# Three results of layer 0's small projections take their buffers from the mixer's rings instead of the ring of raw weights

## The chip, the cores and the metric

The kernel runs on one core of one Trainium2 chip. The metric is the time of one execution in microseconds (us); each kernel's figure is a median of several runs. Before the change it is 3133.64 us (three runs, 3126.05 to 3135.7).

## The reference

A two-layer encoder trunk over 1024 time steps and 1024 channels, all in float32. Layer 0 mixes with two recurrent head groups, layer 1 with banded attention; after each comes an MLP and a gated embedding. The change lies in layer 0's mixer. This is what matters of it:

```python
h = rmsnorm(x, norm_mix_g[i]); proj = h @ even_w_in[e]; dh = token_shift(h) - h
xw, xa, xg = [h + dh * mu_lora[j] for j in range(3)]
w_log = -softplus(-(w0 + tanh(xw @ w1) @ w2)) - 0.5          # rwkv decay
a = sigmoid(a0 + (xa @ a1) @ a2);  g = sigmoid(xg @ g1) @ g2
beta = sigmoid(beta_logit)                                    # columns of proj, 4 heads
gd = -exp(a_log) * softplus(alpha_logit + dt_bias)            # columns of proj, 4 heads
```

The products `xw @ w1`, `xa @ a1` and `xg @ g1` are the low-rank ("lora") products. Since `dh` is a shifted `h` minus `h`, each is computed as `h @ ((1 - mu) * w)` plus the shifted result of `h @ (mu * w)`. The second of these is the "second low-rank product".

## The kernel before, in words

**Tiling.** Channels lie on the 128 partitions, time on the free axis, and layer 0 takes time in two halves of 512 steps. A dense product is 8 blocks of 128 input channels; each block is three TensorE matmuls of 128x512 (high weights by high and low activations, then low weights by high activations), so a product is 24 matmuls into one PSUM bank (`dps`; `dense_part`, L324). Its evacuation multiplies by the row scale on VectorE.

**Weights.** A raw weight tile is 128x1024 and comes by a DMA on SP's queue (L297). `split_w` (L300) turns it into a high part on ScalarE (`whi`, L303) and a low part on VectorE (`wlo`, L304). Raw tiles have the tag `wraw` in the pool `wp`, a ring of **two** slots. A new tile takes the older slot, and what writes it waits until the last reader of the tile there is done.

**Units.** `l0_in` (L567 on) runs 16 units u: four rwkv and four delta-net ("gdn") units in turn for each half. A unit has three or four dense products for its projections, whose results go to the ring `raw` (six slots). In the first unit of each half (u = 0 and u = 8) come in addition, in this order of code: the low-rank pair `la` (decay and a), after the projections `gdn_scalars` (the eight beta and decay logits) and the low-rank pair `lg` (gate). `lora` (L684) loads `lraw`, multiplies it on GpSimd by `1 - mu` and by `mu` (L697, two `wraw` tiles), splits both, and runs two dense products. The second goes through `project` (L670) into `sb`; GpSimd adds it to the first (L706). `gdn_scalars` (L709) clears a `wraw` tile on GpSimd (L712), loads the eight columns, splits, runs a product of which 8 rows count (`ba`, L715), transposes `ba` on TensorE (L192), and computes beta and the decay `gs_g` on VectorE in about thirty small steps (L722 to L749). The cumulative sums (`gdn_cum`, L759) need `gs_g`.

**The chain of a unit.** `rwkv_front` (L799): mixes of raw with its shifted self (`mix`, L807 on ScalarE and L808 on VectorE), two small matmuls from `lao` (`tp`), tanh (L826 and L828), scan (L833), exponentials, `AR` (L864), `Bt` (L865), then score matmuls, then their scaling into `N` on ScalarE (L883), and `inverse_start`, whose substitution runs on GpSimd after two trips through DRAM (L396 to L418). `rwkv_front` takes its temporaries from the ring `f` (11 slots).

**What sets the order.** A planner (`run`, with the table `LAT`) interleaves the generators and so sets the order of emission; its inputs do not change here. Then the framework's scheduler, which simulates the program, fixes the order on each engine. Each engine runs its instructions in that order, and an instruction that waits holds all that stand behind it on its engine. A ring's slots decide what an instruction may wait for, so moving a tile from one ring to another changes waits and, by the scheduler, the order.

Of the kernel before, what the change touches and what calls it, by code (L numbers as in the profile page):

```python
# [8 lines left out]
F32 = mybir.dt.float32  # L9
# [8 lines left out]
P = 128  # L18
# [91 lines left out]
class Trunk:  # L110
# [573 lines left out]
    def lora(self, i, mus, key):  # L684

        nc, a = self.nc, self.a
        om, _ = _VOFF["mulora"]
        raw = self.wp.tile([P, 1024], F32, tag="wraw", name="lraw")
        nc.sync.dma_start(out=raw, in_=a["lora1"][i])

        ws = []
        for src in (self.dv["omul"], self.vecs[:, om:om + 24]):
            w = self.wp.tile([P, 1024], F32, tag="wraw", name="wraw")
            wv = w.rearrange("p (k c) -> p k c", k=NK)
            rv = raw.rearrange("p (k c) -> p k c", k=NK)
            for (c0, c1, j) in mus:
                nc.gpsimd.tensor_tensor(wv[:, :, c0:c1], rv[:, :, c0:c1],  # L697
                                        src[:, 8 * j:8 * j + 8].rearrange("p (k o) -> p k o", o=1)
                                        .broadcast_to((P, NK, c1 - c0)), op=ALU.mult)
            ws.append(w)  # L700
        out = (self.l0 if key == "lg" else self.fr).tile([P, HB], F32, tag=key + "o", name=key + "o", bufs=2 if key == "lg" else 1)
        wa, wb = [self.split_w(w) for w in ws]
        yield from self.dense_half(wa, lambda ps: nc.vector.tensor_tensor(out, ps, self.rs, op=ALU.mult))
        sb = self.wp.tile([P, 1024], F32, tag="wraw", name="sb")
        yield from self.project(wb, key, 1, raw=sb)
        nc.gpsimd.tensor_tensor(out, out, sb[:, 0:HB], op=ALU.add)  # L706
        return out

    def gdn_scalars(self, hf, sc):  # L709
        nc, a, l0 = self.nc, self.a, self.l0  # L710
        raw = self.wp.tile([P, 1024], F32, tag="wraw", name="wraw")
        nc.gpsimd.memset(raw, 0.0)  # L712
        nc.sync.dma_start(out=raw.rearrange("p (k c) -> p k c", k=NK)[:, :, 0:8], in_=a["wba"])
        ba = self.wp.tile([P, 1024], F32, tag="wraw", name="ba")
        yield from self.dense_half(self.split_w(raw), lambda ps: nc.vector.tensor_tensor(ba[0:8, 0:HB], ps[0:8], self.rs[0:8],  # L715
                                                                                         op=ALU.mult))
        yield "gdn_scalars0"
        pt = self.bank()
        for i in range(4):
            self.tr(pt[:, 8 * i:8 * i + 8], ba[0:8, i * P:(i + 1) * P], self.ident[0:8, 0:8])  # L720
        bat = self.sm.tile([P, 4, 8], F32, tag="bat", name="bat")
        nc.vector.tensor_copy(bat.rearrange("p i c -> p (i c)"), pt[:, 0:32])  # L722
        sh = [P, 4, 4]

        def new(nm):
            return self.sm.tile(sh, F32, tag="gs_" + nm, name="gs_" + nm)
        sc["beta"] = new("beta")
        nc.scalar.activation(sc["beta"], bat[:, :, 0:4], AF.Tanh, scale=0.5)
        V = nc.vector
        V.tensor_scalar(sc["beta"], sc["beta"], 0.5, 0.5, op0=ALU.mult, op1=ALU.add)  # L730
        y, ab, u = new("y"), new("ab"), new("u")
        V.tensor_tensor(y, bat[:, :, 4:8], self.hv[:, 1:2, :].broadcast_to(sh), op=ALU.add)

        V.tensor_scalar(ab, y, -1.0, None, op0=ALU.mult)
        V.tensor_tensor(ab, y, ab, op=ALU.max)
        nc.scalar.activation(u, ab, AF.Exp, scale=-1.0)
        V.tensor_scalar(ab, u, 2.0, None, op0=ALU.add)
        V.reciprocal(ab, ab)
        s, s2, poly = new("s"), new("s2"), new("poly")
        V.tensor_tensor(s, u, ab, op=ALU.mult)  # L740
        V.tensor_tensor(s2, s, s, op=ALU.mult)
        V.tensor_scalar(poly, s2, 2.0 / 17, 2.0 / 15, op0=ALU.mult, op1=ALU.add)
        for n in (13, 11, 9, 7, 5, 3, 1):
            V.tensor_tensor(poly, poly, s2, op=ALU.mult)
            V.tensor_scalar(poly, poly, 2.0 / n, None, op0=ALU.add)
        V.tensor_tensor(poly, poly, s, op=ALU.mult)
        V.scalar_tensor_tensor(poly, y, 0.0, poly, op0=ALU.max, op1=ALU.add)
        sc["g"] = new("g")
        V.scalar_tensor_tensor(sc["g"], poly, -1.0, self.ea.broadcast_to(sh), op0=ALU.mult, op1=ALU.mult)  # L749
        self.mark(("g", hf), self.lat["gdn_scalars1"])  # L750
# [1351 lines left out]
```

## Time and profile before

| | before |
|---|---|
| median of the runs | 3133.64 us |
| the profiled execution | 3130.04 us, of which the span is 3128.3 us |
| TensorE busy, clock granted | 3000.5 us (96%), 0.968 |
| VectorE, ScalarE, GpSimd busy | 2234.1 us, 1510.6 us, 532.5 us |
| layer 0's mixer | about 0 to 880 us of the span |
| its tail with the MLP | about 880 to 1700 us |
| attention | about 1700 to 2300 us |
| second tail | about 2300 to 3128 us |

Rows of a timeline give start, length, engine, line, operation, output and inputs, shape, count, and in brackets the idle time just before and what ended it. A "PEld" is a weight load, which overlaps matmuls. Line numbers are those of the kernel before; after L704 the changed kernel's are one lower.

### The profile page before, as it was taken

The numbers are of one execution on the slowest core, as the hardware profiler recorded it, in microseconds if no ns is written. First come the engines' busy times: TensorE is split into PE (matmuls) and PEld (weight loads), VectorE is DVE, ScalarE is ACT, GpSimd is POOL, SyncE is SP. The second block draws the span as 40 slices with busy tenths as digits, with TensorE's granted clock in tenths as the row PEclk, the third lists the DMA queues.
The fourth block names the chain that finished last, engine by engine and source line by source line (L and its number), as shares of the span: only waits on it lengthen the run. The fifth ranks groups of instructions, "written<-read, shape, count | busy, mean of one in ns | idle before, by whom it ended". The sixth has DMA issues, their size and how long they took to land.

```text
span 3128.3 us, 47113 instructions
## 1 busy us (share of the span) xinstructions
PE 3000.5 (96%) x17288; PEld 2476.6 (79%) x17288; DVE 2234.1 (71%) x4518; ACT 1510.6 (48%) x2922; POOL 532.5 (17%) x978
## 2 busy tenths in 40 slices
PE   7999999999999999999999898999899999999999
PEld 5777777777777788888888888988888788888887
DVE  6646675667758688888866576777768788888862
ACT  4323442434426544444433577777766544444431
POOL 6524443434510000000005210111110000000002
PEclk8989999999999999999999999999999999999999
DMA  3212112212346444754433211110156444654433
GB/s 130 77 43 69 47 44 79 63 56 64 105 159 205 151 152 148 247 177 151 130 108 118 68 36 33 46 35 19 67 181 205 152 155 148 239 182 149 135 107 103
DMA packets 187639, 358.45 MB, mean 115 GB/s; under 512 B 45712, under 2 KB 47888, under 8 KB 187408
## 3 DMA queue, kind: packets, MB, share of 16 engines
q1 hardware_dynamic: 158608, 303.00, 29.9%
q10 hardware_dynamic: 28800, 52.44, 4.4%
q8 instruction: 136, 2.23, 0.3%
q14 instruction: 95, 0.78, 0.1%
HBM read 262.04 MB, written 93.32 MB: 114 GB/s over the span
## 4 chain that ended last, share of the span: by engine, by line
PE 79%; DVE 10%; ACT 4%; DMA 3%; issue 2%; POOL 1%; SPq 0%; DVEq 0%; ACTq 0%; POOLq 0%
PE dps L177 67%; PE ch L177 2%; PE pm L177 1%; PE po L177 1%; PE tp L177 1%; PE iz L177 1%; DVE ptile L350 1%; PE pt L192 1%; DVE f L1058 1%; PE sn L177 1%; PE py L177 1%; DVE pb L1942 1%; ACT pb L1955 1%; DVE wlo L304 1%; POOL subt L415 1%
## 5 line engine op out<-in xcount | busy, mean ns | idle before, releaser
L177 PE MATMUL dps<-r,act 128*128 128x512 f32 x3528 | 831.5, 393 | 0.0
L177 PEld LDWEIGHTS dps<-r,act 128*128 128x128 f32 x3528 | 665.0, 189 | 146.7
L177 PE MATMUL dps<-xg,whi 128*128 128x512 f32 x1280 | 439.1, 424 | 16.6 <-ACT xg L352 7.4
L1599 POOL TENSOR_TENSOR pn<-pn,prs 128x512 f32<-128x512 f32 x32 | 45.5, 1424 | 1578.2 <-ACT prs L386 1481.8
L177 PE MATMUL dps<-wq,act 128*128 128x384 f32 x1536 | 306.3, 345 | 7.7 <-DVE vs L1851 3.7
L177 PEld LDWEIGHTS dps<-xg,whi 128*128 128x128 f32 x1280 | 238.1, 198 | 67.8 <-ACT xg L352 7.4
L177 PEld LDWEIGHTS dps<-wq,act 128*128 128x128 f32 x1536 | 267.2, 192 | 12.1 <-DVE vs L1851 6.1
L177 PE MATMUL dps<-xg,wlo 128*128 128x512 f32 x640 | 261.5, 410 | 1.9 <-DVE wlo L304 1.9
L177 PE MATMUL dps<-late,act 128*128 128x512 f32 x960 | 229.3, 392 | 0.0
L177 PEld LDWEIGHTS dps<-late,act 128*128 128x128 f32 x960 | 180.3, 188 | 39.7
L1272 ACT CAST act<-act 128x512 fp32r<-128x512 f32 (+1 forms) x223 | 137.7, 648 | 129.5 <-PE dps L177 67.4
L1375 DVE TENSOR_TENSOR late<-late,dps 128x512 f32<-128x512 f32 x224 | 152.3, 684 | 62.1 <-PE dps L177 53.7
L1272 ACT CAST act<-late 128x512 fp32r<-128x512 f32 x210 | 124.3, 618 | 136.2 <-PE dps L177 89.3
L177 PE MATMUL dps<-act 128*128 128x512 f32 x672 | 165.2, 392 | 0.0
L1273 DVE TENSOR_TENSOR act<-act 128x512 fp32r<-128x512 f32 (+1 forms) x223 | 155.0, 722 | 5.9 <-ACT act L1272 5.7
L303 ACT CAST whi<-wraw 128x1024 fp32r<-128x1024 f32 x78 | 81.6, 1047 | 154.1 <-PE dps L177 90.3
L177 PEld LDWEIGHTS dps<-xg,wlo 128*128 128x128 f32 x640 | 125.9, 197 | 33.2 <-DVE wlo L304 4.1
L1273 DVE TENSOR_TENSOR act<-late,act 128x512 fp32r<-128x512 f32 x210 | 141.3, 687 | 11.2 <-ACT act L1272 9.3
L177 PEld LDWEIGHTS dps<-act 128*128 128x128 f32 x672 | 126.2, 188 | 28.7
L1507 DVE TENSOR_TENSOR xw<-xw,dps 128x512 f32<-128x512 f32 x174 | 118.0, 683 | 32.4 <-PE dps L177 32.2
L177 PE MATMUL dps<-xw,act 128*128 128x512 f32 x576 | 138.5, 391 | 0.0
L1380 ACT ACTIVATE late<-late 128x512 f32<-128x512 f32 x128 | 80.2, 629 | 118.4 <-DVE late L1375 112.0
(484 smaller groups left out, 5656.2 us busy)
## 6 DMA issues: line engine op xcount, KB each, us to landing
hb<-late ACTq DMA_DIRECT2D x168, 256.0 KB
act<-hb SPq DMA_DIRECT2D x138, 256.0 KB
late<-in_w SPq DMA_DIRECT2D x60, 512.0 KB
wraw<-in_w_in SPq DMA_DIRECT2D x56, 512.0 KB
act<-in_w SPq DMA_DIRECT2D x96, 256.0 KB
braw<-hb SPq DMA_DIRECT2D x72, 256.0 KB
wraw<-in_w_out SPq DMA_DIRECT2D x21, 512.0 KB
wraw<-in_w_qkv SPq DMA_DIRECT2D x21, 512.0 KB
```

What stands on the lines that cost most here:

```text
L177: return self.begin(self.nc.tensor.matmul(out, lhsT, rhs, start=start, stop=stop, skip_group_check=again))
L192: return self.begin(self.nc.tensor.transpose(out, in_, ident))
L303: nc.scalar.copy(hi, raw)
L304: nc.vector.tensor_tensor(lo, raw, hi.bitcast(F32), op=ALU.subtract)
L350: nc.vector.tensor_tensor(dst[:, 1, sl], src, dst[:, 0, sl].bitcast(F32), op=ALU.subtract)
L415: E.tensor_tensor(o, X[:, 0:i, i:i + 1].broadcast_to((NP, i, n)), Bq[:, i:i + 1, i + 1:16].broadcast_to((NP, i, n)), op=ALU.mult)
L1272: A.copy(hi, s)
L1273: V.tensor_tensor(lo, s, hi.bitcast(F32), op=ALU.subtract)
L1375: V.tensor_tensor(r, t, u, op=ALU.add)
L1380: A.activation(t, t, AF.Relu)
L1507: V.tensor_tensor(x[n][:, hs[hf]], x[n][:, hs[hf]], ps, op=ALU.add)
L1599: G.tensor_tensor(pn, pn, prs[:, sl], op=ALU.mult)
```

## The change

```diff
@@ lora
         wa, wb = [self.split_w(w) for w in ws]
         yield from self.dense_half(wa, lambda ps: nc.vector.tensor_tensor(out, ps, self.rs, op=ALU.mult))
-        sb = self.wp.tile([P, 1024], F32, tag="wraw", name="sb")
-        yield from self.project(wb, key, 1, raw=sb)
+        sb = yield from self.project(wb, key, 1)
         nc.gpsimd.tensor_tensor(out, out, sb[:, 0:HB], op=ALU.add)
@@ gdn_scalars
-        ba = self.wp.tile([P, 1024], F32, tag="wraw", name="ba")
+        ba = self.t2()
```

`sb` becomes a tile of the ring `raw` (513 columns, six slots), `ba` one of the ring `f` (11 slots). In each half the ring `wraw` so has three tiles fewer (`sb` of `la`, `ba`, `sb` of `lg`), the ring `raw` two more, the ring `f` one more. No instruction is added or removed.

The scheduler then orders the program anew. From the first instruction to the product of the logits TensorE's order is the same. Behind it, still in unit 0, stand these rows. On **TensorE** (`tp<-lao` the matmuls from the first low-rank pair, `ba` and later `f` the logits, `hsel` a column sum for unit 0), before:

```order
L177 MATMUL tp<-lao,wa_292 128x512 x2
L192 MATMUL dps<-ident,ba 128x8 x4
L177 MATMUL tp<-hsel,f 128x2 x4
L177 MATMUL dps<-xg,whi 128x512 x2
L177 MATMUL dps<-xg,wlo 128x512
```

and now:

```order
L177 MATMUL tp<-lao,wa_292 128x512 x2
L177 MATMUL tp<-hsel,f 128x2 x4
L192 MATMUL dps<-ident,f 128x8 x4
L177 MATMUL dps<-xg,whi 128x512 x2
L177 MATMUL dps<-xg,wlo 128x512
```

The transposes of the logits still stand ahead of the first product of `lg` (`dps<-xg`), behind `hsel` now. On **VectorE** at the same place (evacuation of the logits L715, now L714; the rest but `gs_` is unit 0's chain), before:

```order
L808 TENSOR_SCALAR f<-raw,vecs,f 128x512
L678 TENSOR_TENSOR sb<-dps,rsbc 128x512
L715 TENSOR_TENSOR ba<-dps,rsbc 8x512
L722 COPY bat<-dps 128x32
L732 TENSOR_TENSOR gs_y<-bat,hv 128x16
L734 TENSOR_SCALAR gs_ab<-gs_y 128x16
L829 TENSOR_SCALAR f<-f 128x512
```

and now, from the splits of both `lg` weights on:

```order
L304 TENSOR_TENSOR wlo<-wraw,whi 128x1024 x2
L853 TENSOR_SCALAR cc<-tp 128x8
L828 TENSOR_SCALAR f<-f 128x512
L854 RECIPROCAL cc<-cc 128x8
L832 TENSOR_SCALAR L<-ones,f 128x128 x4
L835 TENSOR_SCALAR m<-L 128x4
L843 TENSOR_TENSOR L<-L,m 128x516
...
L863 TENSOR_SCALAR AR<-f,E 128x4x128
L714 TENSOR_TENSOR f<-dps,rsbc 8x512
L807 TENSOR_SCALAR f<-raw,vecs,f 128x512
L721 COPY bat<-dps 128x32
```

The evacuation of the logits has moved behind unit 0's chain up to `AR`, and all `gs_` steps behind that. On **ScalarE**, where unit 0's scores are scaled into `N`, before:

```order
L894 COPY bh<-f 128x512
L303 COPY whi<-wraw 128x1024
L883 ACTIVATE N<-tp,cc 128x128 x8
L774 ACTIVATE gs_egc<-gs_gc 128x16
L776 ACTIVATE gs_ekd<-gs_gl 128x16
```

and now:

```order
L893 COPY bh<-f 128x512
L735 ACTIVATE gs_u<-gs_ab 128x16
L882 ACTIVATE N<-tp,cc 128x128 x8
L303 COPY whi<-wraw 128x1024
L906 COPY b<-tp 128x512
```

The split of unit 1's first weight (`whi`) stood ahead of `N` and stands behind it now. The splits of the `lg` weights moved up as well: one stands ahead of `tanh` of `lao`, the other between the two tanh of unit 0 (L825 and L827). On SP's queue the load of `lg`'s `lraw` stood behind three loads of `x` and stands ahead of them now, and unit 1's first weight follows those three. On GpSimd the two multiplications for `lg` moved up among the sums of squares (L665), ahead of unit 0's `k2` (now L858); and the copy that starts unit 1's third `raw` tile (L676), which needs the slot of unit 0's second, also stands ahead of `k2`, with two L665 between.

Outside unit 0 the order changes throughout the rest of layer 0's mixer and, in the same kind of small swaps, in the attention, none of whose code is touched; TensorE's order in the first tail is the same.

## The prediction

> **What bounds the kernel now.** I read the page first, then the stages, then the start of layer 0, where the edited tiles live.
>
> ```profile
> span 3128.3 us, 47113 instructions
> PE 3000.5 (96%) x17288; PEld 2476.6 (79%) x17288; DVE 2234.1 (71%) x4518; ACT 1510.6 (48%) x2922; POOL 532.5 (17%) x978
> PE 79%; DVE 10%; ACT 4%; DMA 3%; issue 2%; POOL 1%; SPq 0%; DVEq 0%; ACTq 0%; POOLq 0%
> ```
>
> TensorE (PE) bounds the kernel: 96% busy, 79% of the chain that ended last. So an edit pays only where it shortens PE's idle time or raises its clock. By stretch (PE first, clock after the engines):
>
> ```profile
> 0.00:85.00 85.00, 63.66 (x262) 48.94 (x263) 50.47 (x95) 35.33 (x63) 48.57 (x111) 0.86 0.36 120
> 85.00:880.00 795.00, 765.20 (x6413) 590.21 (x6412) 518.88 (x1172) 304.02 (x637) 333.14 (x734) 0.93 0.22 68
> 395.00:531.00 136.00, 130.37 (x1094) 100.03 (x1093) 89.47 (x220) 48.18 (x101) 55.97 (x116) 0.93 0.20 58
> 1700.00:2300.00 600.00, 545.79 (x3350) 507.95 (x3349) 418.54 (x1308) 417.09 (x972) 92.12 (x90) 0.97 0.16 53
> ```
>
> The first 85 us leave PE idle for 21.3 us; the second half's place of the same code (395 to 531) for 5.6 of 136; attention for 54.2. Two gaps of the start touch the ring of raw weights:
>
> ```profile
> 48.47 1.05 PE L177 MATMUL tp<-hsel,f 128*128 128x2 f32 x8 [0.43 <-ACT f L826]
> 55.42 1.22 PE L177 MATMUL dps<-xg,whi 128*128 128x512 f32 x2 [5.90 <-ACT whi L303]
> 57.26 0.80 PE L177 MATMUL dps<-xg,wlo 128*128 128x512 f32 x1 [0.62 <-DVE wlo L304]
> 67.08 0.49 PE L177 MATMUL py<-AR,Sh 128*128 128x128 f32 x2
> 72.48 1.22 PE L177 MATMUL tp<-bh,blkr 128*128 128x512 f32 x2 [4.91 <-ACT N L883]
> 76.08 1.20 PE L177 MATMUL dps<-xg,whi 128*128 128x512 f32 x2
> ```
>
> Gap one (5.9 us) waits for the first `lg` weight. Gap two (4.9 us) waits for `N`. What stood before them on the other queues:
>
> ```profile
> 47.13 0.42 SPq L689 DMA_DIRECT2D lraw<-in_lora  x1
> 52.38 1.92 POOL L697 TENSOR_TENSOR wraw<-lraw,d_omul 128x1024 f32<-128x1024 f32 x1 [3.05 <-DVE L L844]
> 54.33 1.04 ACT L303 CAST whi<-wraw 128x1024 fp32r<-128x1024 f32 x1 [2.47 <-POOL wraw L697]
> 66.74 6.28 SPq L297 DMA_DIRECT2D wraw<-in_w_in  x2
> 70.34 1.04 ACT L303 CAST whi<-wraw 128x1024 fp32r<-128x1024 f32 x1 [6.18 <-DMA wraw<-in_w_in]
> 71.30 2.17 ACT L883 ACTIVATE N<-tp,cc 128x128 f32<-128x128 f32 x8
> ```
>
> Gap one is `lraw` (issued at 47.13), multiplied at 52.38, split at 54.33. Gap two is ScalarE standing 6.2 us on a weight that SP could only ask for at 66.74, when the second `lg` weight had left its slot, with `N` queued behind. Each gap also costs clock afterwards:
>
> ```profile
> 50.00:52.00 2.00, 0.00 (x0) 0.00 (x0) 2.00 (x11) 0.42 (x2) 0.00 (x0) 0.50 1.00 387
> 62.00:64.00 2.00, 2.00 (x7) 1.52 (x7) 2.00 (x3) 0.46 (x1) 1.59 (x3) 0.65 0.00 0
> 64.00:66.00 2.00, 2.00 (x18) 1.49 (x18) 2.00 (x6) 0.16 (x1) 0.67 (x1) 1.00 0.00 0
> 78.00:80.00 2.00, 2.00 (x6) 1.59 (x5) 0.00 (x0) 0.00 (x0) 0.00 (x0) 0.50 0.11 11
> 80.00:82.00 2.00, 2.00 (x13) 1.75 (x12) 0.00 (x0) 0.19 (x1) 0.00 (x0) 0.88 0.23 22
> ```
>
> The granted clock is 0.50 soon after PE stops and full again only between 62 and 64, and between 80 and 82: about 6 us after dense work came back at 57.26, about 5 after 76.08.
>
> **The change, part by part.** Nothing is added or removed, so the sum is made of waits and order.
>
> *Gap one.* Three tiles leave the two-slot ring. The second `lraw` no longer waits behind `ba`'s predecessors, and on SP it now precedes three loads of `x`; both its products and splits then lie before 50 us. But the transposes of the logits stand ahead of the product that wants these weights, and their evacuation now stands on VectorE behind unit 0's chain up to `AR`. So the wait changes its name. How long it lasts comes from these rows:
>
> ```profile
> 46.67 0.68 DVE L715 TENSOR_TENSOR ba<-dps,rsbc 8x512 f32<-8x512 f32 x1 [4.75 <-PE dps L177]
> 47.73 0.69 ACT L826 ACTIVATE f<-tp,d_ha 128x512 f32<-128x512 f32 x1 [1.68 <-PE tp L177]
> 48.31 0.68 ACT L828 ACTIVATE f<-tp,d_hw 128x512 f32<-128x512 f32 x1
> 50.05 1.36 DVE L833 TENSOR_TENSOR_SCAN L<-ones,f 128x128 f32<-128x128 f32 x4
> 51.75 0.63 DVE L844 TENSOR_TENSOR L<-L,m 128x516 f32<-128x516 f32 x1
> 52.51 2.06 DVE L857 TENSOR_SCALAR f<-f,d_hka,d_omka 128x512 f32<-128x512 f32 x1
> 54.65 1.42 DVE L954 SCALAR_TENSOR_TENSOR Sh<-Sr,ee,blk 128x128 f32<-128x128 f32 x1
> 56.00 1.21 DVE L304 TENSOR_TENSOR wlo<-wraw,whi 128x1024 fp32r<-128x1024 f32 x1
> 57.13 0.41 DVE L860 TENSOR_SCALAR f<-f 128x512 f32<-128x512 f32 x1
> 59.25 0.68 DVE L864 SCALAR_TENSOR_TENSOR AR<-f,E 128x512 f32<-128x512 f32 x1
> ```
>
> ScalarE's first tanh starts at 47.73 as now; a split of 1.04 follows it, so the split of VectorE (1.21) ends at about 50.6. Behind it stand a few column steps (about 0.5 together), a 0.41 (the first `f`), the scan 1.36, `m` about 0.2, 0.63, three copies of about 0.15, L857, L954, a 0.41 and `AR` 0.68. L857 is the same kind of instruction as L860 (0.41) and took 2.06 beside GpSimd's multiplication; L954 is a quarter of `AR`'s size and took 1.42. With 0.41 and 0.35 for these two `AR` ends near 55.6, with the rows as they are near 58.3. The evacuation adds 0.68 and the transposes about 0.4: PE's dense work returns between 56.7 and 59.4, against 57.26 now, with 1.2 us of it done ahead of that. GpSimd stands at that time at the copy for unit 1's third `raw` tile, which waits for the mix behind the evacuation, so little runs beside VectorE. I take 57, a **loss of 1 us** (bounds: 0.6 to 3.4).
>
> The rows also show the pair directly:
>
> ```profile
> 38.26 1.29 POOL L665 TENSOR_TENSOR acc<-acc,xr 128x512 f32<-128x512 f32 x1
> 38.29 2.35 DVE L304 TENSOR_TENSOR wlo<-wraw,whi 128x1024 fp32r<-128x1024 f32 x1 [1.01 <-ACT whi L303]
> ```
>
> A split that began with a GpSimd addition took 2.35 instead of 1.21. The Trainium skill, "SBUF — State Buffer", section "Who interferes with whom", says that a VectorE instruction with two SBUF inputs and a GpSimd one that reads SBUF exclude each other for a whole instruction. By that rule, with GpSimd standing at its copy, the lower bound holds; by the rows alone either could. The trace agrees with the rule.
>
> *The copy that holds GpSimd.* Its queue holds two additions (1.29 each) and `k2`, so `k2` comes about 57.5 + 0.2 + 2.6 + 1.3 = 61.6, and `Bt`, which follows on VectorE, near 63. PE needs it for the scores only after 22 matmuls of `lg`: at the half clock about 9 us, with recovery as now near 63 about 8 us, so near 65. The copy is hidden by the dense work; without that cover it would cost some 4 us.
>
> *Gap two.* PE's scores come about 1 us later than now, so `py` ends near 68.6. `N` no longer stands behind the weight's split: it starts with the scores, at about 67, lasts 2.17 and frees the bank near 69.2. The 4.9 us become about 0.6. What is late next is `gs_g`: PE needs it ahead of the second `lg` product, and its chain of small steps now stands behind everything of unit 0.
>
> ```profile
> 73.12 0.17 DVE L749 SCALAR_TENSOR_TENSOR gs_g<-gs_poly,ea 128x16 f32<-128x16 f32 x1
> ```
>
> Some 25 steps of about 0.17 to 0.2 us one after the other are 5 us; from about 66.5 they end near 72, just when PE has finished the matmuls between (`tp<-bh` 1.2, the two `pm` and `cent` about 2). Bounds: ready at 71 to 74. The second `lg` product then starts near 73 instead of 76.08: a **gain of 3 us** (0.5 to 4.5, the loss at gap one being in it).
>
> *Clock.* Now the product from 76.08 runs its first 4 us at 0.50, which loses 2 us. With a gap below 1 us, or two of about 1 us among small matmuls, between nothing and all of this goes: I take **1 us** (0 to 2). The Trainium skill, "TensorE: Matmul & The Clock Gate", section "The HAM clock gate", has the clock fall after about 3.4 us without work and return after about 3.4 us of it. By that rule all 2 us would be gained and the total would be 1 us lower; the trace's recovery was slower, 5 to 6 us, so I go by the rows.
>
> *Unit 1 on.* Its first weights are loaded and split well before 73, so the dense stream goes on; unit 0's substitution starts from an `N` that is 4 us earlier. The lead of 4 us is kept.
>
> *Second half.* The same three tiles leave the ring at u = 8, where PE idles only 5.6 us in 136: **1 us** of gain (-2 to 3).
>
> *The rest of the order.* In layer 0 after 85 us PE idles 29.8 us, in attention 54.2. The swaps there have no direction that I can read off: **0**, with bounds of a fifth of these 84 us either way, that is 17.
>
> Sum against the profiled execution's 3130.04: -3 - 1 - 1 = -5, so 3125. The median shown, 3133.64, lies 3.6 above that execution; against it the forecast is **3128.6**.
>
> **The rivals.** (1) *The lead grows*: no clock loss after either gap, `AR` without any neighbour, and the second half gives its 3: 4.5 + 2 + 3, and some 4 us from the swaps, is 13.5, so 3120. For it: both gaps do start at this ring. Against: gap one stays. (2) *The swaps in attention cost more than the start gains.* PE waits there for the probabilities:
>
> ```profile
> PE po L177 <- ACT ptile L349: 7.8, 10, 1.8
> PE pt L192 <- DVE ptile L350: 5.2, 12, 1.0
> ```
>
> In the new order pairs of transposes stand in places directly behind the scores, with fewer dense matmuls between. If PE's 54.2 us of idle time there rise by two fifths (22 us), the total is +17, so 3150. It decides from 14.4 us on (5 given back and 9.4 more). For it: each such wait is about 0.5 to 0.8 us, and thirty more would do. Against: matmuls were moved both ways. (3) *The change does nothing for PE*: gap one takes its upper bound, `gs_g` comes at 74, and the second half gives nothing: -0.5, so 3133.
>
> **How the numbers follow.** A measurement of this kernel can tell about 0.3% (9.4 us) from no change. Chances: forecast 0.40, (1) 0.22, (2) 0.30, (3) 0.08. So faster 0.22, same 0.48, slower 0.30. The predicted time is 3128.6; its own case spans 3124 to 3138. The range takes in most of (1) and (2): 3112 to 3154.
>
> **What would show it.** Right: `lraw` of `lg` issued before 40; PE's wait at gap one put down to the logits' evacuation or its transposes, with dense work back near 57; no wait for `N` above 1.5 us; the second `lg` product at 72 to 74; `gs_g` near 72. Wrong: dense work back after 60, a wait for `gs_g` above 2 us, or the clock at 0.50 between 74 and 80. If the total differs by more than 9 us with a start as forecast, the stretch 1700 to 2300 or 85 to 880 holds the difference as idle time or clock of PE.

## The result, and the profile after

The changed kernel takes **3119.79 us** (median of five runs, 3115.08 to 3121.0); five runs of the kernel before beside it have a median of 3133.64 (3126.05 to 3136.78). The ratio is 0.9963 with a 95% interval of 0.9949 to 0.9977: **faster by 0.37%**, some 12 to 14 us. A second comparison with the same code (`again`, below) gave 0.9951 (0.9933 to 0.9970). The forecast was 3128.6, the size is that of rival (1).

From the page of the changed kernel, whose profiled execution took 3119.22 us:

```profile
span 3117.5 us, 47104 instructions
PE 2998.6 (96%) x17288; PEld 2477.6 (79%) x17288; DVE 2222.7 (71%) x4518; ACT 1512.2 (49%) x2922; POOL 534.0 (17%) x978
PE 81%; DVE 9%; ACT 4%; DMA 3%; issue 1%; POOL 1%; SPq 0%; DVEq 0%; POOLq 0%; ACTq 0%
```

TensorE's busy time is the same within 2 us, and the span is 10.8 us shorter. By stretch, as before:

```profile
0.00:85.00 85.00, 66.51 (x284) 51.50 (x285) 49.37 (x97) 37.03 (x64) 56.39 (x118) 0.90 0.41 132
85.00:880.00 795.00, 765.05 (x6435) 591.08 (x6433) 512.01 (x1171) 305.38 (x637) 326.13 (x728) 0.93 0.22 68
395.00:531.00 136.00, 130.46 (x1138) 102.94 (x1138) 86.62 (x217) 49.13 (x101) 51.84 (x108) 0.93 0.19 56
1700.00:2300.00 600.00, 549.41 (x3369) 511.64 (x3369) 419.81 (x1321) 420.88 (x980) 88.75 (x87) 0.96 0.17 56
```

In the first 85 us TensorE is idle 18.5 us where it was 21.3, and its clock is 0.90 instead of 0.86. Attention has 50.6 us of idle time where it had 54.2.

**Gap one** first. On TensorE:

```profile
50.13 1.05 PE L177 MATMUL tp<-hsel,f 128*128 128x2 f32 x8
59.92 0.59 PE L192 MATMUL dps<-ident,f 8*128 8x8 f32 x4 [8.74 <-DVE f L714]
60.44 1.22 PE L177 MATMUL dps<-xg,whi 128*128 128x512 f32 x2
```

The wait is now put down to the logits' evacuation (L714), as forecast, but it lasts 8.7 us where it was 5.9. On the other queues, in order of the cause:

```profile
33.54 0.35 SPq L689 DMA_DIRECT2D lraw<-in_lora  x1
49.35 1.89 POOL L697 TENSOR_TENSOR wraw<-lraw,vecs 128x1024 f32<-128x1024 f32 x1
51.28 1.05 ACT L303 CAST whi<-wraw 128x1024 fp32r<-128x1024 f32 x1 [1.21 <-POOL wraw L697]
52.36 1.32 DVE L304 TENSOR_TENSOR wlo<-wraw,whi 128x1024 fp32r<-128x1024 f32 x1 [5.47 <-ACT whi L303]
53.68 1.40 DVE L828 TENSOR_SCALAR f<-f 128x512 f32<-128x512 f32 x1
57.48 0.54 DVE L856 TENSOR_SCALAR f<-f,d_hka,d_omka 128x512 f32<-128x512 f32 x1
58.00 0.34 DVE L953 SCALAR_TENSOR_TENSOR Sh<-Sr,ee,blk 128x128 f32<-128x128 f32 x1
58.60 0.69 DVE L863 SCALAR_TENSOR_TENSOR AR<-f,E 128x512 f32<-128x512 f32 x1
59.20 0.67 DVE L714 TENSOR_TENSOR f<-dps,rsbc 8x512 f32<-8x512 f32 x1
```

`lraw` is asked for at 33.5 instead of 47.1. But GpSimd multiplies it for the second weight only at 49.35, behind sums of squares and the low-rank addition, and VectorE stands 5.47 us at the split of that weight with unit 0's chain and the evacuation queued behind. From the split's end (53.68) to that of `AR` (59.29) it takes 5.6 us where my lower end had 5.0: L857 (now L856) takes 0.54 and L954 (now L953) 0.34, as that end had it, but L828 takes 1.40 instead of 0.41.

**Gap two** is gone:

```profile
69.69 2.18 ACT L882 ACTIVATE N<-tp,cc 128x128 f32<-128x128 f32 x8 [2.89 <-PE tp L177]
71.35 0.71 PE L177 MATMUL tp<-bh,blkr 128*128 128x512 f32 x2
72.70 0.17 DVE L748 SCALAR_TENSOR_TENSOR gs_g<-gs_poly,ea 128x16 f32<-128x16 f32 x1
74.25 0.71 PE L177 MATMUL dps<-xg,whi 128*128 128x512 f32 x2
```

and the clock there, by slices as before:

```profile
74.00:76.00 2.00, 2.00 (x13) 1.69 (x12) 1.12 (x4) 1.09 (x4) 0.00 (x0) 1.00 0.21 31
```

TensorE waits no more for `N` (no bracket at 71.35), `gs_g` is there 1.0 us before its matmuls (73.89), and the second `lg` product runs at the full clock from 74.25, where it ran at half from 76.08. That full clock belongs to this profile: in two other profiles of the changed kernel (`again` and `after_d`, below) the product begins earlier, at 72.84 and 73.18, and the clock from 74 to 76 us is 0.55 and 0.61.

### The profile page after: what moved, and what is told of

Read it like the earlier page. It is cut to its first block, busy times and chain, and to the rows that moved or that the text cites. A ratio compares the mean times of both kernels' runs of the same rounds, so it can differ in the third digit from the quotient of the medians.

```text
span 3117.5 us, 47104 instructions
## 1 busy us (share of the span) xinstructions
PE 2998.6 (96%) x17288; PEld 2477.6 (79%) x17288; DVE 2222.7 (71%) x4518; ACT 1512.2 (49%) x2922; POOL 534.0 (17%) x978
## 4 chain that ended last, share of the span: by engine, by line
PE 81%; DVE 9%; ACT 4%; DMA 3%; issue 1%; POOL 1%; SPq 0%; DVEq 0%; POOLq 0%; ACTq 0%
PE dps L177 68%; PE ch L177 2%; PE po L177 2%; PE iz L177 1%; PE pm L177 1%; PE tp L177 1%; PE pt L192 1%; DVE ptile L350 1%; PE py L177 1%; PE sn L177 1%; DVE pb L1941 1%; ACT pb L1954 1%; PE pp L177 1%; DMA wraw<-in_w_out 1%; PE st L177 1%
## 5 line engine op out<-in xcount | busy, mean ns | idle before, releaser
L1374 DVE TENSOR_TENSOR late<-late,dps 128x512 f32<-128x512 f32 x224 | 152.3, 684 | 62.5 <-PE dps L177 54.2
```

Of the source, the lines that this page charges most:

```text
L1374: V.tensor_tensor(r, t, u, op=ALU.add)
```

## How the lead is followed through the program

A time at the end doesn't say where it was won. The evacuations of layer 0's dense products come in a fixed order, so the start of the same evacuation in two traces gives the lead (how much earlier it comes) at that point. One reading is good to a few us only, since the work around an evacuation is ordered anew: the changed kernel's first profile reads 4.2 at 102.6 us, -1.2 at 109.0 and 2.6 at 128.4. This table is worked out from VectorE's rows, in us against the first profile of the kernel before, at the times given there. The later columns are experiments, told below. The last two rows are span, and time at the half clock from the trace's clock records (about 2 us of it behind the last instruction).

| at | after | again | after_c | after_d | before_b | before_c | half0 | half1 | sb_only | ba_only |
|---|---|---|---|---|---|---|---|---|---|---|
| 84.8 | 4.8 | 4.8 | 5.0 | 4.8 | -0.3 | 0.5 | 6.2 | 0.6 | -0.2 | 1.7 |
| 102.6 | 4.2 | 4.4 | 4.4 | 4.4 | -0.3 | 0.5 | 5.9 | 0.6 | -0.2 | -0.6 |
| 205.4 | 4.5 | 16.7 | 4.8 | 17.1 | 1.1 | 1.9 | 18.5 | 0.8 | -0.7 | 5.4 |
| 444.5 | 6.0 | 17.0 | 6.4 | 17.3 | 4.1 | 1.3 | 18.9 | 1.5 | 4.9 | 14.3 |
| 662.6 | 7.5 | 18.6 | 7.9 | 18.8 | -7.5 | -10.4 | 20.2 | 4.8 | -1.2 | 13.0 |
| 801.4 | 4.3 | 11.6 | 5.5 | 15.7 | -9.4 | -12.0 | 10.5 | 0.7 | -13.0 | 4.5 |
| span | 3117.5 | 3117.0 | 3117.9 | 3103.7 | 3134.7 | 3137.1 | 3114.4 | 3117.9 | 3129.8 | 3114.2 |
| half clock | 202.9 | 179.4 | 190.0 | 156.1 | 206.7 | 216.4 | 172.0 | 183.5 | 200.6 | 172.4 |

(The first profile of before: span 3128.3, half clock 203.2.) The first two rows repeat within 0.2 us in the four profiles of the changed kernel. Further on the same code differs by 12 us from one execution to the next, and so does the kernel before.

## The experiments

**One tile at a time.** `sb_only` makes the low-rank half of the change, `ba_only` the logits' half:

```diff
@@ sb_only, against before
-        sb = self.wp.tile([P, 1024], F32, tag="wraw", name="sb")
-        yield from self.project(wb, key, 1, raw=sb)
+        sb = yield from self.project(wb, key, 1)
@@ ba_only, against before
-        ba = self.wp.tile([P, 1024], F32, tag="wraw", name="ba")
+        ba = self.t2()
```

> Only the low-rank results move to the raw ring; the logits stay in wraw. If the slots of wraw make the gain at the start (first theory): lraw of lg is still asked for late and gap one stays near 6 us with dense work back near 55.5, but unit 1's weight is early, the wait for N falls below 1 us, the second lg product starts near 72, and the lead over the kernel before at 130 to 300 us is 4 us or a little more, since gap one does not grow. If the gain came from the new order of rows instead (second theory): TensorE's order up to the second lg product is the old one here, so gap two stays at 4 to 5 us and the lead at 130 us is below 1.

> Only the logits move to the f ring. First theory (slots of wraw): lg's weights come early, gap one is put down to the logits' evacuation and lasts 8 to 9 us with dense work back at 59 to 60; N stands behind a split of a weight on ScalarE still, so some of gap two stays (1 to 4 us); lead at 130 us between -1 and 3. Second theory (any new order gives the same): lead near 4 us as with the whole change.

Measured: `sb_only` 3126.62 us, ratio 0.9993 (0.9982 to 1.0005); `ba_only` 3115.17 us, ratio 0.9958 (0.9938 to 0.9978). TensorE in `sb_only`:

```profile
57.00 1.22 PE L177 MATMUL dps<-xg,whi 128*128 128x512 f32 x2 [4.50 <-ACT whi L303]
69.89 0.72 PE L177 MATMUL tp<-bh,blkr 128*128 128x512 f32 x2 [0.15 <-ACT N L882]
73.83 1.16 PE L177 MATMUL pm<-AR,b 64*128 64x128 f32 x4 [3.21 <-DVE PMQ L931]
75.79 1.20 PE L177 MATMUL dps<-xg,whi 128*128 128x512 f32 x2
```

and in `ba_only`:

```profile
58.27 0.59 PE L192 MATMUL dps<-ident,f 8*128 8x8 f32 x4 [6.79 <-DVE f L715]
69.04 0.72 PE L177 MATMUL tp<-bh,blkr 128*128 128x512 f32 x2 [0.43 <-ACT N L883]
71.81 0.92 PE L177 MATMUL pm<-AR,b 64*128 64x128 f32 x4 [2.05 <-DVE PMQ L932]
```

The ring's part is shown: with TensorE's order unchanged up to 80 us, and the split of unit 1's weight still ahead of `N` on ScalarE (but at 66.66, without a wait), `sb_only` cuts the wait for `N` from 4.91 to 0.15. But the lead I expected from it (4 us) did not come. This execution was 3.0 us behind at 34.8 us (1.4 from a later start of its first products, the rest from a fall of the clock at 19 us), had made them good and 2.6 more when it reached `tp<-bh`, and gives most of that back in a new wait directly behind, 3.2 us for `PMQ` (masked scores that VectorE writes, L932). `ba_only` has the longer gap one, 6.79 us and not the 8 to 9 expected; its wait for `N` is gone too, against my 1 to 4, and it pays 2.05 for `PMQ`. In the whole change the first profile shows no such wait, and `again` 1.28 us. The lead of `ba_only` is -0.6 at 102.6 us, but 1.7 at 128.4 (expected: -1 to 3), where the whole change has 2.6 to 3.0, and 4.3 at 168.2, where that has 3.5 to 4.5; `sb_only` has -0.2 and -1.8 there. So from 168 us on the logits' half alone has the lead of the whole change or more, and the low-rank half has none, though it removes the wait for `N`. As a whole, too, `ba_only` is as fast as the full change.

**One half at a time.** `half0` makes the change for u = 0 alone, `half1` for u = 8 alone:

```diff
@@ half0, against before (half1 has 1 for 0)
-        sb = self.wp.tile([P, 1024], F32, tag="wraw", name="sb")
-        yield from self.project(wb, key, 1, raw=sb)
+        sb = self.wp.tile([P, 1024], F32, tag="wraw", name="sb") if self.hf != 0 else None
+        sb = yield from self.project(wb, key, 1, raw=sb)
-        ba = self.wp.tile([P, 1024], F32, tag="wraw", name="ba")
+        ba = self.t2() if hf == 0 else self.wp.tile([P, 1024], F32, tag="wraw", name="ba")
```

(One more line, not shown, stores `hf` in `self.hf`.)

> The change in the first half only (u = 0). First theory: the start is that of the changed kernel row by row, lead 4 us at 300 us, and no further gain at the second half's site: 4 (2 to 5) at 531 us as well. Second theory (gain spread over all by the swaps): lead below 2 or above 6 at 300 us, or the gain at 395 to 531 us appears without the change there. Whole: 3124 to 3131 by the first.

> The change in the second half only (u = 8). First theory: nothing before 300 us (lead 0 within 0.5), and 2 to 4 us won between 395 and 531 us. Second theory (the site is not what won there): lead below 1 at 531 us or a gain that sits outside 395 to 531. Whole: 3128 to 3133 by the first; half0 and half1 add up to the whole change within 4 us by the first, not by the second.

Measured: `half0` 3125.21 us, ratio 0.9994 (0.9979 to 1.0008); `half1` 3124.07 us, ratio 0.9989 (0.9977 to 1.0). At the start `half0` has the lead of the whole change and 1.5 us more, `half1` none, so the start's gain belongs to the first half. (At 296 us `half0` leads by 17.1, not 4: the step from 102.6 to 205.4 is explained below.) Between the evacuations at 392.1 and 539.1 us, which enclose the second half's site, `half1` wins 1.9 us, a little less than expected, and `half0`, without the change there, 1.2; the whole change wins 2.7 to 3.0, but `before_b` and `before_c` lose 2.0 and 2.8 with the code of before. In `half1` the second `lraw` is asked for at 445.3 instead of 480.3, as with the whole change (441.0). Still, TensorE's idle time at the site hardly differs: 5.3 us in 136 against 5.6. The two ratios add up to a gain of 5 us, the whole change makes 12 to 15: more than the 4 us apart that the first theory allowed, though the intervals are as wide as the gap. For the whole that theory is not borne out; for the start it holds.

**The same kernels again.** `again` is the changed kernel, timed anew; `before_b`, `before_c`, `after_c` and `after_d` are single executions with a profile.

> The changed kernel itself once more, for a second profile, to tell what is the order's and what is one execution's. If the lead of 4 us between 395 and 531 us and the gap one of 8.7 us come from the order, both are there again within 1 us, and the start is 1.5 us earlier if the clock does not fall at 19 us this time. If the 5 us won behind 1000 us (the start of the MLP, attention) are the order's, they return; if they are one execution's, they come out between -3 and 8. Whole: 3115 to 3124, ratio 0.995 to 0.998.

> The kernel before once more, for its profile alone. In its first profile TensorE's clock was 0.50 from 172 to 199 us, among small matmuls, and 13.5 us were lost there; the second profile of the changed kernel lacks this. If the fall belongs to the order of before, it is there again with 13 to 14 us; if to the one execution, it may be absent and the dense products after 205 us then come 10 to 13 us earlier.

> As the run above, a third profile of the kernel before. By the first reading (order) the fall at 172 to 199 us is there a third time; by the second (execution) two of three or one of three.

> The changed kernel, a third profile. By the reading that the fall of the clock at 165 to 200 us belongs to the execution, it is there or not with the same rows in the same order, and idle time of TensorE before 130 us is the same as in the two others within 0.5 us; gap one 8.7 us again. Lead at the fourth dense product of unit 1 (102.6 us in the kernel before): 4 to 6 us.

> The changed kernel, a fourth profile: as the run above. Dense products at 444 us of the kernel before lead by 5 to 7 us where the fall at 165 to 200 us took place in both, by 16 to 19 where it did not in the changed kernel.

Measured: `again` 3115.69 us, ratio 0.9951 (0.9933 to 0.9970); `before_b` 3136.46, `before_c` 3138.76, `after_c` 3119.6, `after_d` 3105.37. The two readings meet in the stretch from 165 to 200 us. The kernel before, first profile; the same in `before_b`; the changed kernel's first; and `again`:

```profile
165.00:200.00 35.00, 34.39 (x328) 25.80 (x328) 10.30 (x25) 6.51 (x17) 11.88 (x38) 0.61 0.15 41
```
```profile
165.00:200.00 35.00, 28.75 (x334) 22.13 (x333) 10.40 (x26) 6.52 (x17) 12.11 (x38) 0.80 0.15 41
```
```profile
165.00:200.00 35.00, 34.01 (x267) 25.41 (x266) 9.38 (x24) 6.16 (x17) 11.84 (x38) 0.61 0.14 39
```
```profile
165.00:200.00 35.00, 33.85 (x368) 25.93 (x366) 15.87 (x42) 8.04 (x19) 12.09 (x39) 1.00 0.17 52
```

With the same code, the granted clock over these 35 us is 0.61 or 1.00 in the changed kernel (`after_c` 0.61; `after_d` 1.00) and 0.61 or 0.80 in the kernel before (`before_c` 0.80). Each time the rows are small matmuls of the same kinds. Four of `pm` take 1.65 us in the kernel before at 176.22, and 0.92 in `again` at 171.19:

```profile
176.22 1.65 PE L177 MATMUL pm<-AR,b 64*128 64x128 f32 x4
```
```profile
171.19 0.92 PE L177 MATMUL pm<-AR,b 64*128 64x128 f32 x4
```

So in the changed kernel the fall there belongs to the execution, and it costs 12 us (the step between the rows 102.6 and 205.4 of the table). The leads of `after_c` and `after_d` at 444.5 us, 6.4 and 17.3, are those expected with the fall and without it.

In the kernel before, the same stretch shows something else. `before_b` and `before_c` ran these matmuls at the full clock up to 185 us and still lead by only 1.1 and 1.9 us at 205.4. What took the time back is a wait of 5.6 us (`before_c` 5.3) at `iz<-T,N`, matmuls of the inverse of an rwkv unit. TensorE in the kernel before, first profile; the same and ScalarE in `before_b`; TensorE in `again`:

```profile
189.58 0.61 PE L177 MATMUL iz<-T,N 32*32 32x16 f32 x28
```
```profile
187.99 0.61 PE L177 MATMUL iz<-T,N 32*32 32x16 f32 x28 [5.60 <-ACT T L442]
187.54 0.40 ACT L442 ACTIVATE T<-Xp,half 128x128 f32<-128x128 f32 x1 [6.61 <-DMA Xp<-z]
```
```profile
182.89 0.73 PE L177 MATMUL dps<-xg,whi 128*128 128x512 f32 x2
194.48 0.23 PE L177 MATMUL iz<-T,N 32*32 32x16 f32 x2
```

`T` follows the substitution on GpSimd and its trip through DRAM, and starts at 187.22 in the first profile and at 187.54 in `before_b`, whatever TensorE's clock was. In the old order `iz<-T,N` stands ahead of the next dense product, so TensorE can't pass this point before 187 to 188 us, and the fall of the clock costs 1 to 2 us only. In the new order the dense product stands first, and an execution that keeps the full clock keeps the 12 us. The other runs agree: `half1` and `sb_only`, which have the old order here, read 0.8 and -0.7 at 205.4; `half0` and `ba_only`, which have the new one, 18.5 without the fall and 5.4 with it. So my expectation of 13 to 14 us lost to the clock in the kernel before was wrong, and so was its rival, 10 to 13 us won without the fall.

Executions of the kernel before differ again at 630 to 660 us (clock 0.89 in its first profile, 0.66 in `before_b` and `before_c`), and there the two lose 6.4 us each against the first (evacuations at 634.2 and 657.4). Behind 801.4 us the first profile of the changed kernel wins 6.5 us; `again` has -0.3 there, `after_c` 4.9, `after_d` 8.9, `before_b` 3.0: so what is won there can't be put down to the order.

What this does to the verdict can be had from all the runs, since each lists its mean clock. In 47 runs of the kernel before beside these experiments the time fell by 1.74 us for each 0.001 of mean clock (correlation -0.83). Their means are 3129.55 us at 0.9693; eleven runs of the changed kernel have 3117.31 us at 0.9703. Of the 12.2 us between them 1.7 go with the clock by that slope, or about 3 if half a microsecond is counted for each at the half clock; **9 to 11 us are there at equal clock**. Against the 17 runs beside it alone, `again` is 15.5 us faster, 4.6 of them with the clock, which is about 11 again. The division is not clean, since an order can bring on a fall by itself: in `before_b` the half clock sets in at 185.8 us, within the wait for `T`.

**The transposes behind `lg`.** Gap one is now the place of the logits' transposes ahead of the `lg` products. `lg_first` moves them and all that follows behind both products, in the changed kernel; `lg_first_ba` does the same in `ba_only`:

```diff
-                yield from self.gdn_scalars(hf, sc)
+                ba = yield from self.gdn_logits(hf)
                 gg = yield from self.lora(1, [(0, 128, 2)], "lg")
+                yield from self.gdn_scalars(hf, sc, ba)
```

(`gdn_logits` is `gdn_scalars` up to the logits' evacuation, and `gdn_scalars` then begins with the transposes.)

> The changed kernel with the logits' transposes and the small steps behind them moved in the code to behind both products of lg. If PE's gap one is only the place of the transposes (first theory): the first lg product starts at 48 to 50 us, the second when its low part is split near 54, no wait above 4 us remains before the scores at 62 to 65, and the clock falls once less: 6 to 9 us ahead of the changed kernel at 130 us, 3111 to 3115 as a whole if the swaps behind give nothing. If unit 0's chain bounds the start (rival): PE waits for the scores or for gs_g instead, 5 to 8 us in one piece, and the lead over the changed kernel at 130 us is below 2.

> The same edit of the code on the kernel in which only the logits move to the f ring. First theory: at 130 us 4 to 9 us ahead of that kernel, 3106 to 3112 as a whole if the rest of the order holds. Rival: lead at 130 us below 2. If the order behind the start decides as much as the start does, the whole differs from the lead at 300 us by more than 5 us either way.

Measured: `lg_first` 3116.03 us, ratio 0.9963 (0.9947 to 0.9979); `lg_first_ba` **3101.75 us, ratio 0.9910 (0.9893 to 0.9927)**, which beats both kernels. TensorE in `lg_first`, all its waits above 0.5 us from 20 to 79 us:

```profile
56.63 0.74 PE L177 MATMUL dps<-xg,whi 128*128 128x512 f32 x2 [1.42 <-DVE lgo L704]
64.83 1.88 PE L177 MATMUL tp<-AR,b 64*128 64x128 f32 x16 [2.08 <-DVE b L869]
```

The 8.7 us are replaced by 1.4 and 2.1. At the evacuations of 102.6 and 128.4 us `lg_first` leads the first profile of before by 9.9 and 12.3, the changed kernel by 4.2 and 2.6: 6 to 10 us ahead, as the first theory wanted at 130 us, and the rival (unit 0's chain gives the time back) falls for these products. Yet the whole of `lg_first` is no faster than the changed kernel: its lead is 19.9 at 444.5 us and 5.7 at 801.4. In `lg_first_ba` it is 11.9 at 102.6, 21.8 at 662.6 and 16.2 at 801.4. Its whole is 31 us under the kernel before by the medians, its lead at 296 us was 8.6: what lies behind the start moves more than the start does, as the last sentence expected of it had allowed. Part of that is clock: its five runs have a mean of 0.9736, those of the kernel before beside them 0.9687, which is 8.5 of the 28 us between the means by the slope above. Why one order keeps the lead and the clock and the other loses them was not settled.

## Why the forecast fell short, step by step

- **Gap one.** Right that the wait changes its name; the place in the queue was right, the time not. The split was to end at 50.6 and ended at 53.7: GpSimd's second multiplication was taken as early, and it had its queue before it. Dense work came back at 60.44 (58.80 in `again`), not 57, past the bound of 59.4 in the first profile. 1.6 us of this come from a fall of the clock at 19 us, which the first profile had and `again` not. The gap itself is 8.7 us in both; `again` gave its 1.6 us back behind it, in the 1.28 us for `PMQ` and at the half clock from 72.4 to 75.8, and both lead by 4.8 at 84.8.
- **The lower end for VectorE.** Right: with GpSimd idle until 58.09, L856 and L953 took 0.54 and 0.34. But a step that I counted at its usual length (0.41) was not: L828 took 1.40 beside GpSimd's sum of squares (it reads one tensor, so the rule in the prediction's words, two inputs, does not cover it).
- **The copy that holds GpSimd.** Wrong: it ran at 51.19 without a wait, and GpSimd's wait of 3.29 us is for L856:

```profile
51.19 0.19 POOL L676 COPY raw<-h_g 128x3 f32<-128x3 f32 x1
58.09 2.31 POOL L858 TENSOR_TENSOR f<-f 128x512 f32<-128x512 f32 x1 [3.29 <-DVE f L856]
```

- **Gap two.** Right in mechanism, and `gs_g` at 72.70 was forecast near 72. The second `lg` product began at 74.25 (forecast 73), 1.8 us earlier than before instead of 3; in `again` it was 3.2.
- **Clock at the start.** 3 + 1 us were forecast for the gaps and the clock, and four profiles have 4.2 to 4.4 at 102.6 us, by errors that cancelled: in the first profile less came from the gaps and all 2 us from the clock, in `again` more from the gaps and less from the clock. The match is in part luck of the place, too: from 114 to 168 us the same four profiles read 1.1 to 4.5.
- **Second half, 1 us.** 2.7 to 3.0 us between 392.1 and 539.1. That these three tiles make it isn't shown, as `half0` wins 1.2 there, and the kernel before differs by as much from itself.
- **The rest of the order, 0.** This term failed. Between 102.6 and 444.5 us, with the same fall of the clock in both, the new order wins 1.8 to 2.0 more (4.2 to 6.0 and 4.4 to 6.4). Over the whole the change makes 9 to 11 at equal clock, of which at most some 7 are the start's and the second half's terms. One part is now known: `iz<-T,N` has moved behind a dense product, which is worth up to 12 us at 205.4 in an execution that keeps the full clock there, and next to nothing in one that does not. It need not last to the end: `again` ends at 3117.0 and `after` at 3117.5, `after_d` at 3103.7. The rest stays open. The sign of the whole term could not have been read off: `sb_only` and `ba_only`, both ordered anew throughout, end 2 and 14 us below the kernel before.
- **The base.** The sum was made against one execution, and the median that the forecast was moved to lies 3.6 above it. Executions of one kernel differ by up to 17 us (3120.92 to 3138.14 in those 47 runs), and the granted clock goes with most of it; the profile that I worked from holds a fall of the clock of 27 us among small matmuls that `before_b` and `before_c` have at half that length (and pay for with the wait for `T`), and has only short ones near 560 and 640 us, where they have long ones.
- **Rival (1)** had the size (3120) but not by its parts: no clock loss after the gaps held only for the second, and there in two of four profiles, and `AR` came near its lower length but late. The time lies within the range only because the range takes in most of this rival; the forecast's own case ended at 3124, and a gain that can be told from no change had been given 0.22. **Rival (2)** did not come: attention's idle time is 50.6 to 53.0 us in the four profiles of the changed kernel and 52.4 to 54.2 in three of the kernel before.
- **What would show it.** Right: `lraw` early, the evacuation named, no wait for `N`, `gs_g`. In the first profile one mark for wrong came, dense work back after 60; in `again` and `after_d` another, the half clock between 74 and 76. All the same all four lead by 4.8 to 5.0 at 84.8, so these two marks did not tell whether the start would gain.

## What to carry to other kernels

A tile in a short ring holds more than its slot: all loads and splits behind it on four queues. When it leaves, look for the wait that stands next in line (here `PMQ` and the logits' transposes), because that and not the removed wait sets the gain. In a kernel that is ordered anew by a scheduler, follow the lead at milestones that can't change their order, at several of them and in several profiles of each side, before a stretch is called won or lost; and compare times at equal clock. Before a fall of the clock is given a price, ask what TensorE would have waited for at full clock: here the same fall is worth 12 us in one order and 1 to 2 in the other.

## What the runs showed of the hardware

In the trace's clock records the half clock comes in whole steps of 3.41 us: 3.41, 6.83, 10.24, 13.65 and 27.31 us in the first 500 us of the kernel before. The Trainium skill, "TensorE: Matmul & The Clock Gate", section "The HAM clock gate", describes a free-running window of 3413 ns, so that its place differs from run to run; the steps agree, and so does that two waits of TensorE between 15 and 20 us brought the clock down in some executions (`after`, 0.65 and 1.04 us; `ba_only`, 0.66 and 0.88) and not in others (the kernel before, 0.55 and 1.04; `after_c`, 0.56 and 1.04). That so little idle time can be enough differs from the 3.4 us without work that the prediction gives from there; here the measurement decides. What I had not expected is that TensorE, busy for 34.4 of 35 us, stayed at the half clock for 27 us among matmuls of 16 to 128 columns and came back only with the dense products. Such a stretch cost 12 us in the changed kernel, which is 96% busy. What lets one execution fall there and spares another was not tried.
